# The last gate of a decoder layer: three of its four 256-column blocks by seven products instead of eight

## The chip, the cores and the metric

The kernel runs on one core of a Trainium2 chip. The metric is the device time of one execution in microseconds. The engines are named as the profile names them: PE multiplies matrices, PEld loads its weights, DVE, ACT and POOL (VectorE, ScalarE, GpSimd) work on elements, SP issues the transfers (DMA).

## The reference

One decoder layer on 1024 tokens with model width 1024: a half feed-forward, two gated attention branches, a second half feed-forward, and at the end the gated per-layer input embedding. Only the end is changed:

```python
x = x + 0.5 * swiglu(rms_norm(x, ffn2_norm[i]), ffn2_w_gate[i], ffn2_w_up[i], ffn2_w_down[i])
x = x + jax.nn.sigmoid(rms_norm(x, ple_norm[i]) @ w_ple_gate[i]) * (p[i] @ w_ple_proj[i])
```

All data are float32. `p @ w_ple_proj` is computed early in the kernel and kept in memory as `p_proj`.

## The kernel before

**Precision.** Every float32 operand is split into a high part, which ACT writes by a cast, and a low part, which DVE writes by a subtraction (`split`, L112 and L113, short: hi and lo). A product is three passes of matmuls: hi by hi, lo by hi, hi by lo. One matmul takes 128 rows of the inner dimension, a weight tile of 128 columns and a moving tile of 512 tokens. Activations lie transposed: features on the partitions, tokens in two halves of 512.

**Seven products.** The feed-forward stages already multiply by Strassen's scheme in Winograd's form. A 1024 x 256 block of weights is cut into 2 x 2 pieces, the activations into 2 x 2 (two halves of the inner dimension, two halves of the tokens), and seven products of 12 matmuls replace eight. `product(n, m)` is product m (1 to 7) of block n; I write (n, m) for it. The sums of weight pieces (L462 to L467) are made on POOL or DVE, the sums of activation pieces (`combo_t`, `combo_u`, `combo_d`) on DVE, and their splits (`combo_l`, `combo_s`, `combo_e`) on ACT and DVE. `prep(n, m)` splits the weight operand of a product four products ahead of its use. The results run together in PSUM banks "b" (products 1, 6, 7, 4), "a" (2) and "d" (5, 3), and `evict` copies and adds them.

**Entry of such a stage.** Block 0 is multiplied by eight plain products (`plain`, L449), since the sums of activations aren't there yet; meanwhile the norm of the second half of the tokens is finished and the combinations are made. Then come (1,1), (1,2), (2,1), (2,2) in `products`, and from (1,5) on the list `seqn`. The second feed-forward enters behind the output projection of attention (`second_entry`), whose last chunk of down products has 12 matmuls per tile, as the last chunk of the second feed-forward has.

**The last gate before.** It is plain: 16 units `ple_steps(u)`, each 128 columns by 512 tokens, 24 matmuls at L1591. A unit ends with a sigmoid on ACT (L1594), a multiplication by `p_proj` (L1595) and an addition of the residual X (L1596) on DVE, and a store of 256 KB. Units 0 to 3 use the first half of the tokens, while the norm of the second half is finished beside them. The low parts of the gate's weights are made on POOL (`wlow`, L146). The residual X stays in its two buffers X until the end. The last unit is done in two halves of 256 tokens.

**Order.** From the feed-forward on, the order on each engine is that of the code (`tc.manual_schedule`), each engine works its list in order, and a wait holds up all that stands behind it on that engine. All transfers are issued by SP in one list. Buffers come from pools with a fixed number of slots (GF, RN and PT 3, H 4, KL, KH, Q, Y and X 2), and a new tile waits for a slot's last user.

Of the kernel before, what the change touches and what calls it, by code (L numbers as in the profile page):

```python
# [38 lines left out]
def tile_hybrid_decoder_layer(  # L39
# [360 lines left out]
    def ffn(N, wg, wu, wd, next_gain, resid, hid, tags, entry, tail):  # L400

        wsrc = [kp(w[0]) for w in (wg, wu)]
        wdown = wd[0].rearrange("(j k p) n -> k p j n", k=2, p=P)
        LA = 4
        nm_ = 2 * NF  # L410
# [58 lines left out]
        def prep(n, m):  # L469
            if m == (6 if n == 3 else 1) and n > 2:  # L470
                sums(n, nc.vector if n == 3 else nc.gpsimd)
                if n == 3:
                    last_sum(n)
# [5 lines left out]
            if m == 2 and n > 3:  # L479
# [27 lines left out]

        def evict(n, m, ps):
            up, j = n % 2, n // 2
            if m == 1:  # L510
                E[n] = [slot(t, [P, 2, 512]) for t in (("GF", "RN"), ("Y", "Y"))[up]]
            e1, e2 = E[n]
            if m == 1:
                nc.scalar.copy(e1[:, 0, :], ps[:])
            elif m == 6:
                nc.scalar.copy(e1[:, 1, :], ps[:])
            elif m == 7:
                nc.scalar.copy(e2[:, 1, :], ps[:])
                nc.vector.tensor_add(e2[:, 1, :], e2[:, 1, :], bank_of[n, "d"][:])
            elif m == 2:  # L520
                nc.vector.tensor_add(e1[:, 0, :], e1[:, 0, :], ps[:])
            elif m == 3:
                nc.vector.tensor_add(e1[:, 1, :], e1[:, 1, :], ps[:])
            if not up:
                if m == 7:
                    nc.scalar.activation(e2[:, 1, :], e2[:, 1, :], AF.Silu)
                elif m == 4:
                    nc.scalar.activation(e2[:, 0, :], ps[:], AF.Silu)
                elif m == 3:
                    nc.scalar.activation(e1[:], e1[:], AF.Silu)  # L530
                return
            g1, g2 = E[n - 1]
            if m == 7:
                nc.vector.tensor_mul(g2[:, 1, :], g2[:, 1, :], e2[:, 1, :])
            elif m == 4:
                nc.vector.tensor_mul(g2[:, 0, :], g2[:, 0, :], ps[:])
                nc.sync.dma_start(hid[j, :, 1:3, :], g2[:])
            elif m == 3:
                nc.vector.tensor_mul(g1[:], g1[:], e1[:])
# [1115 lines left out]
```

## Time and profile before

| | us |
|---|---|
| median of 3 runs | 2234.41 (2233.1 to 2235.34) |
| the profiled execution | 2233.62, its span 2231.9 |
| PE / DVE / ACT / POOL busy | 2222.2 / 1489.1 / 970.8 / 811.8 |
| first matmul of the last gate | 2138.14 |
| start of its last two matmuls | 2227.48 |
| first matmul of the second feed-forward (L449) | 1503.00 |

The profile is one execution. Its page gives busy times, the chain of work that ended last, and groups of instructions; the timeline gives instructions in order of time, merged where the same ones follow each other: start, length, engine, line, operation, output and inputs by tile names, count, and in brackets the idle time before and what ended it. ps are PSUM banks, names ending in _dram and p_proj, x_mix, hidden lie in memory. A row of several merged instructions runs from the first one's start to the last one's end; instructions of one engine overlap a little, so the distance from start to start says more than the length.

### The profile page before, as it was taken

What the parts mean: (1) busy time and instruction counts of PE and PEld (TensorE: products, weight loads), DVE (VectorE), ACT (ScalarE), POOL (GpSimd) and SP (SyncE); (2) the same over time, 40 slices, a digit from 0 to 9 for tenths busy, and PEclk for the clock granted to TensorE, in tenths of its full rate; (3) what the DMA queues carried; (4) which work ended last, traced back from release to release, by engine and by line L of the source; (5) the groups of instructions that cost most, each with busy time, mean ns of one, the idle gap of its engine ahead of it and who ended that gap; (6) DMA issues with size and microseconds to landing.
All of it is one profiled execution on the core that took longest, in us unless ns stands there. A gap on an engine that the chain in (4) does not pass through costs nothing.

```text
span 2231.9 us, 29977 instructions
## 1 busy us (share of the span) xinstructions
PE 2222.2 (100%) x11241; PEld 1886.6 (85%) x11241; DVE 1489.1 (67%) x2188; ACT 970.8 (43%) x1694; POOL 811.8 (36%) x709
## 2 busy tenths in 40 slices
PE   9999999999999999999999999999999999999999
PEld 7888888888889999898988888887888888888887
DVE  7955545497894565656666676899654555778873
ACT  6433333343444555545456564255333333434441
POOL 0254444310014656645455654400644443200111
PEclk9999999999999999999999999999999999999999
DMA  8232332474433222222124236741423232655132
GB/s 321 90 123 90 105 108 95 156 286 148 151 129 90 58 86 67 77 62 77 39 71 119 62 124 215 260 143 56 142 94 119 85 128 80 252 201 203 66 118 90
DMA packets 187521, 278.08 MB, mean 125 GB/s; under 512 B 27752, under 2 KB 109928, under 8 KB 187376
## 3 DMA queue, kind: packets, MB, share of 16 engines
q1 hardware_dynamic: 187376, 276.17, 36.8%
q8 instruction: 88, 1.44, 0.3%
q14 instruction: 57, 0.47, 0.1%
HBM read 192.47 MB, written 75.27 MB: 120 GB/s over the span
## 4 chain that ended last, share of the span: by engine, by line
PE 90%; DVE 4%; ACT 2%; issue 2%; DMA 1%; POOL 0%; SPq 0%; DVEq 0%; ACTq 0%; POOLq 0%
PE ps L496 36%; PE ps L388 18%; PE ps L762 11%; PE ps L754 7%; PE ps L1236 4%; PE ps L1591 4%; PE ps L1026 3%; PE ps L1004 2%; PE ps L449 2%; PE ps L953 1%; PE ps L952 1%; ACT H L112 0%; DMA PT<-in_x_tokens_dram 0%; DVE H L113 0%; DVE H L273 0%
## 5 line engine op out<-in xcount | busy, mean ns | idle before, releaser
L388 PE MATMUL ps<-H,H 128*128 128x512 f32 x2184 | 497.3, 389 | 0.0
L388 PEld LDWEIGHTS ps<-H,H 128*128 128x128 f32 x2184 | 409.5, 188 | 84.8
L496 PE MATMUL ps<-H,WL 128*128 128x512 f32 x1008 | 238.9, 389 | 0.0
L496 PEld LDWEIGHTS ps<-H,WL 128*128 128x128 f32 x1008 | 189.2, 188 | 39.3
L762 PE MATMUL ps<-H,WH 128*128 128x512 f32 x768 | 209.5, 401 | 0.0
L762 PEld LDWEIGHTS ps<-H,WH 128*128 128x128 f32 x768 | 136.4, 188 | 22.4
L1007 DVE TENSOR_TENSOR PT<-ps,PT 128x512 fp32r<-128x512 f32 (+1 forms) x160 | 100.4, 633 | 73.7 <-ACT PT L1006 72.8
L146 POOL TENSOR_TENSOR WL<-RAW,WH 128x512 fp32r<-128x512 f32 (+1 forms) x104 | 123.8, 1211 | 63.4 <-ACT WH L136 46.5
L496 PE MATMUL ps<-H,Q 128*128 128x512 f32 x576 | 137.4, 389 | 0.0
L396 DVE SCALAR_TENSOR_TENSOR X<-ps,X 128x512 f32<-128x512 f32 x168 | 108.5, 682 | 41.9 <-PE ps L388 41.8
L754 PE MATMUL ps<-WH,H 128*128 128x256 f32 (+1 forms) x896 | 131.7, 286 | 0.2 <-DVE log_f L793 0.2
L496 PEld LDWEIGHTS ps<-H,Q 128*128 128x128 f32 x576 | 108.1, 188 | 22.4
L1006 ACT CAST PT<-ps 128x512 fp32r<-128x512 f32 (+1 forms) x160 | 86.8, 549 | 85.0 <-PE ps L1004 83.4
L754 PEld LDWEIGHTS ps<-WH,H 128*128 128x128 f32 x896 | 117.2, 190 | 1.1 <-PE ps L754 0.3
L496 PE MATMUL ps<-X,WL 128*128 128x512 f32 x480 | 115.6, 390 | 0.0
L209 POOL TENSOR_TENSOR PT<-PT,RN 128x1024 f32<-128x1024 f32 x2 | 4.8, 2402 | 295.1 <-ACT RN L203 295.1
L762 PE MATMUL ps<-H,WL 128*128 128x512 f32 x384 | 108.7, 399 | 0.0
L1026 PE MATMUL ps<-PT,X 128*128 128x256 f32 (+1 forms) x640 | 106.0, 283 | 1.6 <-DVE PT L1007 1.0
L1026 PEld LDWEIGHTS ps<-PT,X 128*128 128x128 f32 x640 | 95.1, 189 | 14.6 <-DVE PT L1007 4.0
L496 PEld LDWEIGHTS ps<-X,WL 128*128 128x128 f32 x480 | 90.0, 188 | 19.1 <-DVE WL L113 0.5
L965 POOL TENSOR_TENSOR T<-T,l 128x128 f32<-128x128 f32 (+3 forms) x64 | 73.2, 1147 | 85.1 <-DVE l L964 85.1
L496 PE MATMUL ps<-H,PT 128*128 128x512 f32 x432 | 103.2, 390 | 0.2 <-DVE PT L113 0.2
(405 smaller groups left out, 4638.1 us busy)
## 6 DMA issues: line engine op xcount, KB each, us to landing
hidden<-PT SPq DMA_DIRECT2D x40, 512.0 KB, 3.1
WH<-in_ffn_w_gate_dram SPq DMA_DIRECT2D x38, 512.0 KB, 5.4
Q<-hidden SPq DMA_DIRECT2D x24, 512.0 KB, 6.5
hidden<-RN SPq DMA_DIRECT2D x22, 512.0 KB, 2.6
RAW<-in_w_in_dram SPq DMA_DIRECT2D x22, 512.0 KB, 3.9
KH<-in_ffn_w_up_dram SPq DMA_DIRECT2D x20, 512.0 KB, 6.1
KL<-in_ffn_w_up_dram SPq DMA_DIRECT2D x20, 512.0 KB, 6.9
T<-in_ffn_w_down_dram SPq DMA_DIRECT2D x20, 512.0 KB, 4.4
```

Of the source, the lines that this page charges most:

```text
L146: ins = eng_lo.tensor_sub(lo[part], raw[part], f(hi[part]))
L388: pe(nc.tensor.matmul(groups[g][t][:], wt[:, b, k, t * P:(t + 1) * P], act[:, a, k, :], start=(fresh and n == 0), stop=(i in (6, 1, 4) and ...
L396: nc.vector.scalar_tensor_tensor(xs, groups[g][t][:], scale, xs, ALU.mult, ALU.add)
L496: pe(nc.tensor.matmul(ps[:], hl[:, a, k, :], rhs(m, b, k), start=(first and i == 0), stop=(final and i == 11), skip_group_check=True))
L754: pe(nc.tensor.matmul(ps[:, :n], hT[t // 4][a][:, k, (t % 4) * P:(t % 4 + 1) * P], w[k // 4][b][:, k % 4, :n], start=(i == 0), stop=(i == ...
L762: pe(nc.tensor.matmul(ps[:], w[a][:, k, :], hT[half][b][:, k, :], start=(i == 0), stop=(i == 23)))
L965: nc.gpsimd.tensor_mul(T[:, :n], T[:, :n], l[:].broadcast_to([P, n]))
L1006: high = nc.scalar.copy(pt[:, 0, :width], ps[:, :width])
L1007: low = nc.vector.tensor_sub(pt[:, 1, :width], ps[:, :width], f(pt[:, 0, :width]))
L1026: pe(nc.tensor.matmul(o, lh, r, start=(kpair == c and i == 0), stop=(kpair == 0 and i == 3)))
L1236: pe(nc.tensor.matmul(ps[:], w[a][:, k, :], yT[g][b][:, k, half * 512:half * 512 + 512], start=(i == 0), stop=(i == 11)))
L1591: pe(nc.tensor.matmul(ps, pl["w"][d, k // 2][b][:, k % 2, m * P:(m + 1) * P], hT[half][a][:, k, cs], start=(i == 0), stop=(i == 23)))
```

## The change

The code that was inside `ffn` moves into `machine` and `run_products`, with the same order for the feed-forwards. The last gate becomes such a stage with four blocks of 256 columns: block 0 plain, blocks 1 to 3 by seven products, 348 matmuls where there were 384 (the last 24 of them cut in two halves of 256 tokens). It enters with `entry_tail`, the second half of `second_entry`.

The X buffers are needed for the combinations, so the residual is written to memory (`x_last`, eight transfers of 512 KB from `finished`, during the last down products) and read back one 128-column row at a time (`fetch_px`), together with the matching row of `p_proj`. A column d of the result is finished by `finish(i)`, with d = ORDER[i]: a product with `p_proj` and a sum with x, over all 1024 tokens at once; for i = 0 to 3 (columns 0, 1, 2, 4) both are on POOL, for the others on DVE (of column 5 one half on POOL). The weight sums of block 3 move from DVE to POOL. `norm_tags` gives the last down products of the second feed-forward the buffers that the output projection uses.

```diff
+    def machine(N, source, nm_, tags, act):
...
         def prep(n, m):
-            if m == (6 if n == 3 else 1) and n > 2:
-                sums(n, nc.vector if n == 3 else nc.gpsimd)
-                if n == 3:
+            if m == (6 if n == 3 and nm_ > 4 else 1) and n > 2:
+                sums(n, nc.vector if n == 3 and nm_ > 4 else nc.gpsimd)
+                if n == 3 and nm_ > 4:
                     last_sum(n)
...
-            if m == 2 and n > 3:
+            if m == 2 and n > 3 - (nm_ == 4):
                 last_sum(n)
...
+    def sequence(nm_):
+        seqn = [(1, 5), (2, 5), (1, 6), (2, 6), (1, 7), (2, 7), (1, 3), (2, 3), (3, 1), (3, 2), (1, 4), (2, 4), (3, 6), (3, 5), (3, 7)]
+        for n in range(4, nm_ - 1):
+            seqn += [(n, 1), (n - 1, 4), (n, 2), (n - 1, 3), (n, 6), (n, 5), (n, 7)]
+        n = nm_ - 1
+        if n > 3:
+            seqn += [(n, 1), (n - 1, 4), (n, 2), (n, 6), (n, 5), (n, 7), (n - 1, 3)]
+        else:
+            seqn.remove((2, 4))
+            seqn.append((2, 4))
+        seqn += [(n, 3), (n, 4)]
+        return seqn, seqn[:7] + [(1, 4), (2, 3), (3, 1), (3, 2)] + seqn[11:]
...
+    def run_products(M, nm_, evict, each):
+        seqn, seqp = sequence(nm_)
+        for s, (n, m) in enumerate(seqn):
+            evict(n, m, M.product(n, m))
+            if s == 0:
+                for q in range(2):
+                    M.s(q, 7)
+            elif s in (1, 5):
+                M.d(s // 5)
+                M.e(0) if nm_ == 4 and s == 5 else None
+            elif s in (6, 7):
+                M.e(s - 6) if s == 7 or nm_ > 4 else None
+            nxt_ = seqp[s + LA] if s + LA < len(seqn) else None
+            if nxt_:
+                M.prep(*nxt_)
+            each(n, m, nxt_)
...
@@ -713,14 +730,14 @@
                     continue
                 if final:
                     if i == 1:
-                        nxt.extend(norm_begin(X[h], next_gain) for h in range(2))
+                        nxt.extend(tail["begin"](X) if "begin" in tail else [norm_begin(X[h], next_gain) for h in range(2)])
...
+    def entry_tail(F, N):
...
-    def ple_steps(u):
...
+    xf = dp.tile([KD, P, S], F32, name="x_last")
+    def last_gate():
+        G = {"E": {}, "px": {}}
+        tags = {"raw": {0: ("RAW", "RAW"), 1: ("WH", "WH"), 2: ("RAW", "RAW"), 3: ("WH", "WH")}, "sum": {1: "WH", 2: "KL", 3: "WH"}, "w": ("Q", "Q", "KH", "KH"), "hl": ("WL", "WL", "WL", "KL") + ("PT",) * 6 + ("WL", "WL", "PT", "WL", "WL", "PT", "WL", "WL", "WL", "PT", "WL", "WL", "PT", "WL", "WL")}
+        wg = kp(w_ple_gate[0])
+        ORDER = (0, 1, 2, 4, 3, 6, 7, 5)
+        def begin(X):
+            G["x"] = X
+            G["n"] = [combo_begin(X[0], 3, True), combo_begin(X[1], 3, False)]
+            G["m"] = machine(G["n"], lambda n, kh: wg[:, 4 * kh:4 * kh + 4, n * 256:n * 256 + 256], 4, tags, AF.Sigmoid)
+            return G["n"]
+        def finished(half, j):
+            nc.sync.dma_start(xf[2 * j:2 * j + 2, :, half * 512:half * 512 + 512].rearrange("k p n -> p k n"), G["x"][half][:, 2 * j:2 * j + 2, :])
+        def fetch_px(tiles, *order):
+            for i, pair in zip(order, tiles):
+                G["px"][i] = pair
+                for a, src in zip(pair, (pd, xf)):
+                    nc.sync.dma_start(a, src[ORDER[i]].rearrange("p (h n) -> p h n", h=2))
+        def couple(i):
+            return [slot(t, [P, 2, 512])[:] for t in (("GF", "RN"), ("KL", "KL"), ("GF", "RN"), ("KL", "KL"))[i]]
+        def room():
+            t = slot("H", [P, 4, 2, 512])
+            return [(t[:, 2 * j], t[:, 2 * j + 1]) for j in range(2)]
+        def store(d):
+            nc.sync.dma_start(out[:, :, d, :].rearrange("h p n -> p h n"), G["m"].E[d // 2][d % 2][:])
+        def finish(i, parts=((slice(0, 2), slice(0, 512)),)):
+            d = ORDER[i]
+            e = G["m"].E[d // 2][d % 2]
+            a, r = G["px"][i]
+            for h, cs in parts:
+                eng = nc.gpsimd if i in (0, 1, 2, 3) or (i == 7 and h == 1) else nc.vector
+                eng.tensor_mul(e[:, h, cs], e[:, h, cs], a[:, h, cs])
+                eng.tensor_add(e[:, h, cs], e[:, h, cs], r[:, h, cs])
+                if isinstance(h, int):
+                    nc.sync.dma_start(out[h][:, d, cs], e[:, h, cs])
+                elif i not in (2, 3):
+                    store(d)
+            if i < 2:
+                fetch_px([couple(i + 2)], i + 2)
+        def evict(n, m, ps):
+            E, bank_of = G["m"].E, G["m"].bank_of
+            if m == 1:
+                E[n] = [slot(t, [P, 2, 512]) for t in (("GF", "RN"), ("Y", "Y"), ("GF", "RN"), ("KH", "Q"))[n]]
+            e1, e2 = E[n]
+            sig = lambda o, i_: nc.scalar.activation(o, i_, AF.Sigmoid)
+            if m == 1:
+                nc.scalar.copy(e1[:, 0, :], ps[:])
+            elif m == 6:
+                nc.scalar.copy(e1[:, 1, :], ps[:])
+            elif m == 7:
+                nc.scalar.copy(e2[:, 1, :], ps[:])
+                nc.vector.tensor_add(e2[:, 1, :], e2[:, 1, :], bank_of[n, "d"][:])
+                sig(e2[:, 1, :], e2[:, 1, :])
+                if n == 3:
+                    finish(ORDER.index(7), ((1, slice(0, 512)),))
+            elif m == 2:
+                nc.vector.tensor_add(e1[:, 0, :], e1[:, 0, :], ps[:])
+            elif m == 5:
+                if n == 3:
+                    sig(e1[:, 0, :], e1[:, 0, :])
+                    finish(ORDER.index(6), ((0, slice(0, 512)),))
+            elif m == 3:
+                nc.vector.tensor_add(e1[:, 1, :], e1[:, 1, :], bank_of[n, "d"][:])
+                if n == 3:
+                    sig(e1[:, 1, :], e1[:, 1, :])
+                    finish(ORDER.index(6), ((1, slice(0, 512)),))
+                else:
+                    sig(e1[:], e1[:])
+                    finish(ORDER.index(2 * n))
+            elif m == 4 and n < 3:
+                sig(e2[:, 0, :], ps[:])
+                if n == 2:
+                    finish(ORDER.index(5), ((1, slice(0, 512)), (0, slice(0, 512))))
+                else:
+                    finish(ORDER.index(2 * n + 1))
+            elif m == 4:
+                parts = [(0, slice(j * 256, j * 256 + 256)) for j in range(2)]
+                for _, cs in parts:
+                    sig(e2[:, 0, cs], ps[:, cs])
+                finish(ORDER.index(7), parts)
+        def each(n, m, ahead):
+            if (n, m) == (1, 5):
+                finish(0)
+            elif (n, m) == (1, 6):
+                finish(1)
+            elif n == 3 and m < 3:
+                fetch_px(room(), 2 * m + 2, 2 * m + 3)
+                store(ORDER[m + 1])
+        def end(X, N):
+            M = G["m"]
+            entry_tail(dict(vars(M), evict=evict), N)
+            for i in range(2):
+                fetch_px([couple(i)], i)
+            run_products(M, 4, evict, each)
+        hooks = {"begin": begin, "late": True, "end": end}
+        def hook(i, t, call):
+            hooks.setdefault((i, t), []).append(call)
+        for i in (1, 4, 5, 6):
+        return hooks
...
     tags = {"raw": {0: ("RAW", "RAW"), 1: ("WH", "WH"), 2: ("RAW", "RAW"), 3: ("WH", "WH"), 4: ("KH", "KL")}, "sum": {1: "WH", 2: "KL", 3: "KL"}, "w": ("Q", "Q", "KH", "KH"), "hl": ("WL", "WL", "WL", "KL") + ("PT",) * 6 + ("WL", "WL", "PT", "WL", "WL", "PT", "WL", "WL", "WL", "PT", "WL", "Q", "Q")}
-    ffn(N, ffn2_w_gate, ffn2_w_up, ffn2_w_down, 3, xm, ad[1], tags, second_entry, tail)
-    for u in range(8, 16):
-        run(ple_steps(u))
+    ffn(N, ffn2_w_gate, ffn2_w_up, ffn2_w_down, 3, xm, ad[1], tags, second_entry, last_gate())
```

On POOL, this is what stood in the last gate before, from the first low parts of the gate's weights on: only subtractions at L146, two halves to a row, and the two powers of the norms.

```order
L146 TENSOR_TENSOR WL_2676_18242<-Y_2669_18170,WH_2675_18240 128x512 x2
L146 TENSOR_TENSOR WL_2678_18247<-Y_2670_18172,WH_2677_18245 128x512 x2
L248 TENSOR_TENSOR rs_2687_18350<-ss_2686_18345,mhalf_84 128x4
L146 TENSOR_TENSOR GF_2696_18417<-RAW_2683_18317,T_2692_18392 128x512 x2
L146 TENSOR_TENSOR RN_2697_18420<-RAW_2684_18319,T_2693_18394 128x512 x2
L248 TENSOR_TENSOR rs_2709_18542<-ss_2708_18537,mhalf_84 128x4
L146 TENSOR_TENSOR WL_2733_18737<-Y_2723_18665,WH_2732_18735 128x512 x2
L146 TENSOR_TENSOR GF_2735_18753<-Y_2724_18667,T_2734_18751 128x512 x2
L146 TENSOR_TENSOR RN_2739_18775<-RAW_2727_18699,T_2738_18773 128x512 x2
L146 TENSOR_TENSOR PT_2741_18791<-RAW_2728_18701,PT_2740_18789 128x512 x2
```

Now, from the power of the second norm to the end of column 4's sum: L1614 and L1615 are the products and sums of columns 0, 1, 2 and 4, with GF, RN and KL as fetched operands; L445 to L450 are the weight sums of block 3.

```order
L248 TENSOR_TENSOR rs_2699_18523<-ss_2698_18521,mhalf_84 128x4
L1614 TENSOR_TENSOR GF_2695_18513<-GF_2695_18513,GF_2736_18752 128x1024
L1615 TENSOR_TENSOR GF_2695_18513<-GF_2695_18513,RN_2737_18753 128x1024
L1614 TENSOR_TENSOR RN_2696_18514<-RN_2696_18514,KL_2738_18756 128x1024
L1615 TENSOR_TENSOR RN_2696_18514<-RN_2696_18514,KL_2739_18757 128x1024
L445 TENSOR_TENSOR WH_2755_18887<-WH_2751_18845 128x512
L446 TENSOR_TENSOR WH_2751_18845<-WH_2751_18845,WH_2752_18846 128x4x128
L447 TENSOR_TENSOR WH_2755_18887<-WH_2751_18845 128x512
L1614 TENSOR_TENSOR Y_2718_18612<-Y_2718_18612,GF_2743_18784 128x1024
L1615 TENSOR_TENSOR Y_2718_18612<-Y_2718_18612,RN_2744_18785 128x1024
L450 TENSOR_TENSOR WH_2752_18846<-WH_2752_18846,WH_2755_18887 128x4x128
L1614 TENSOR_TENSOR GF_2724_18650<-GF_2724_18650,KL_2748_18825 128x1024
```

The four subtractions per half of the weights are gone, and eight operations on 128 x 1024 elements stand there, the first four ahead of the weight sums of block 3.

On SP before, in the middle of the gate: rows of `p_proj`, the weights of the second 512 columns, and stores.

```order
L1576 DMA KL_2712_18578<-p_proj_88 128x2x512
L1597 DMA out_0_dram<-Q_2713_18580 128x512
L1597 DMA out_0_dram<-KH_2718_18624 128x512
L1576 DMA KL_2720_18657<-p_proj_88 128x2x512
L126 DMA Y_2723_18665<-in_w_ple_gate_dram 128x2x512
L126 DMA Y_2724_18667<-in_w_ple_gate_dram 128x2x512
L1597 DMA out_0_dram<-Q_2721_18659 128x512
L126 DMA RAW_2727_18699<-in_w_ple_gate_dram 128x2x512
```

Now, from the first fetched row to the weights of block 3 (WH): each row of `p_proj` with its row of `x_last`, and the stores of columns 0 and 1.

```order
L1596 DMA GF_2736_18752<-p_proj_88 128x1024
L1596 DMA RN_2737_18753<-x_last_13398 128x1024
L1596 DMA KL_2738_18756<-p_proj_88 128x1024
L1596 DMA KL_2739_18757<-x_last_13398 128x1024
L1606 DMA out_0_dram<-GF_2695_18513 128x2x512
L1596 DMA GF_2743_18784<-p_proj_88 128x1024
L1596 DMA RN_2744_18785<-x_last_13398 128x1024
L1606 DMA out_0_dram<-RN_2696_18514 128x2x512
L1596 DMA KL_2748_18825<-p_proj_88 128x1024
L1596 DMA KL_2749_18826<-x_last_13398 128x1024
L413 DMA WH_2751_18845<-in_w_ple_gate_dram 128x4x256
L413 DMA WH_2752_18846<-in_w_ple_gate_dram 128x4x256
```

The weights of block 3 stand behind four fetched pairs and two stores. In the list of waits KL_2739 takes the slot of KL_2738 and waits for the product of column 1 on POOL, the store of RN_2696 waits for column 1's sum on POOL, and KL_2749 waits for the low part WL_2746 on DVE.

On DVE before, the gate had a product and a sum per unit:

```order
L1595 TENSOR_TENSOR Q_2713_18580<-Q_2713_18580,KL_2702_18494 128x512
L1596 TENSOR_TENSOR Q_2713_18580<-Q_2713_18580,X_2525_16991 128x512
L273 TENSOR_TENSOR H_2654_18024<-PT_2716_18602,H_2653_18023 128x1024
L273 TENSOR_TENSOR H_2654_18024<-Q_2717_18614,H_2653_18023 128x1024
L1595 TENSOR_TENSOR KH_2718_18624<-KH_2718_18624,KL_2702_18494 128x512
L1596 TENSOR_TENSOR KH_2718_18624<-KH_2718_18624,X_2525_16991 128x512
```

Now, in the stretch of (1,5) to (2,7), from the last sum of activations of `combo_u(1)` on: L113 are low parts (WL_2734 of (1,6), H_2731 of the activations of m = 6, WL_2735 of (2,6), X_2741 of m = 7, PT_2742 of (1,7), WL_2746 of (2,7)), L450 weight sums, L537 and L538 `combo_d(0)`.

```order
L528 TENSOR_TENSOR KH_2715_18576<-KH_2715_18576,RN_2683_18378 128x1024
L113 TENSOR_TENSOR WL_2734_18742<-WH_2726_18653,WL_2734_18742 128x512
L113 TENSOR_TENSOR H_2731_18708<-KH_2715_18576,H_2731_18708 128x1024
L113 TENSOR_TENSOR WL_2735_18747<-KL_2729_18678,WL_2735_18747 128x512
L450 TENSOR_TENSOR WH_2692_18465<-WH_2692_18465,WH_2726_18653 128x4x128
L450 TENSOR_TENSOR RAW_2702_18530<-RAW_2702_18530,KL_2729_18678 128x4x128
L113 TENSOR_TENSOR X_2741_18773<-Q_2705_18552,X_2741_18773 128x1024
L113 TENSOR_TENSOR X_2741_18773<-Q_2714_18573,X_2741_18773 128x1024
L113 TENSOR_TENSOR PT_2742_18778<-WH_2726_18653,PT_2742_18778 128x512
L537 TENSOR_TENSOR Q_2705_18552<-H_2652_18023,KH_2707_18558 128x1024
L538 TENSOR_TENSOR Q_2705_18552<-Q_2705_18552,H_2652_18023 128x1024
L113 TENSOR_TENSOR WL_2746_18803<-KL_2729_18678,WL_2746_18803 128x512
```

All of them stand in one list, and the low parts of (1,7) and (2,7) come behind the combinations for m = 6, 7 and 4.

More of the change, by code (lines that the diff above doesn't have):

```diff
@@ L506, in right @@
             return t[:, b, k, :]
[L508 to L539, printed above, removed]
-                nc.sync.dma_start(hid[j, :, 0, :], g1[:, 0, :])
-        def hidden_sums(n, tags):
-            j = n // 2
-            block_sums(hid[j], *E[n - 1], tags)
-            del E[n], E[n - 1]
         C = {}
```

145 lines of the change are left out of this document (62 added, 83 removed).

## Prediction

> **What bounds it now.** The page first: PE is busy over the whole span.
>
> ```profile
> PE 2222.2 (100%) x11241; PEld 1886.6 (85%) x11241; DVE 1489.1 (67%) x2188; ACT 970.8 (43%) x1694; POOL 811.8 (36%) x709
> ```
>
> So what counts is how many matmuls the gate has and whether PE waits. The windows compare the gate (second row) with the entry of the second feed-forward (first row), which the changed gate copies. In the gate DVE is busy 40.7 of 89.9 us; in the entry 58.31 of 62.00, and POOL does nothing there (1.01).
>
> ```profile
> 1503.00:1565.00 62.00, 61.41 (x269) 48.92 (x268) 58.31 (x74) 31.33 (x47) 1.01 (x1) 1.00 0.25 79
> 2138.10:2228.00 89.90, 89.04 (x417) 73.91 (x416) 40.70 (x53) 23.72 (x40) 12.64 (x9) 1.00 0.35 116
> ```
>
> Then PE's timeline in the gate, from its first matmul to its last two.
>
> ```profile
> 2138.14 1.07 PE L1591 MATMUL ps<-H,WH 128*128 128x512 f32 x4
> ...
> 2140.40 0.74 PE L1591 MATMUL ps<-H,T 128*128 128x512 f32 x2 [0.74 <-ACT H L270]
> ...
> 2156.69 1.07 PE L1591 MATMUL ps<-H,WH 128*128 128x512 f32 x4
> ...
> 2162.13 1.07 PE L1591 MATMUL ps<-H,WH 128*128 128x512 f32 x4
> ...
> 2227.48 0.40 PE L1591 MATMUL ps<-H,PT 128*128 128x256 f32 x2
> ```
>
> A unit of 24 matmuls takes 2162.13 - 2156.69 = 5.44 us, one matmul 0.227. The gate lasts from 2138.14 to 2227.88, 89.7 us, with one wait of 0.74.
>
> **Matmuls.** The changed gate is the entry of the second feed-forward, row for row, as far as (1,5), and then 17 products of 12 matmuls. PE's timeline there:
>
> ```profile
> 1503.00 2.88 PE L449 MATMUL ps<-H,WL 128*128 128x512 f32 x12
> 1506.27 3.22 PE L449 MATMUL ps<-H,WL 128*128 128x512 f32 x12 [0.39 <-ACT WL L112]
> ...
> 1522.89 4.98 PE L496 MATMUL ps<-H,PT 128*128 128x512 f32 x20 [0.20 <-DVE PT L113]
> ...
> 1538.60 5.60 PE L496 MATMUL ps<-H,PT 128*128 128x512 f32 x24
> 1544.04 5.60 PE L496 MATMUL ps<-H,WL 128*128 128x512 f32 x24
> 1549.47 2.88 PE L496 MATMUL ps<-X,PT 128*128 128x512 f32 x12
> 1552.19 3.02 PE L496 MATMUL ps<-X,WL 128*128 128x512 f32 x12
> 1555.05 5.63 PE L496 MATMUL ps<-T,WL 128*128 128x512 f32 x24
> ```
>
> I count t from the gate's first matmul, which answers to 1503.00. (1,5) starts at t = 35.6, its waits of 0.39 and 0.20 included; 17 products of 2.72 (1552.19 - 1549.47) are 46.2; with 0.2 for the last one's end the gate lasts 82.0. That is **7.7 us less** than 89.7; the old wait of 0.74 and the copied ones of 0.59 are in the two lengths, and so are the norm's transposes, as many in each. The eight stores to x_last cost nothing: the stores to x_mix stand at the same places in front of 1503.00, and PE waits there no longer than shown; without that cover the first loads of weights, which stand behind them in SP's list, would be late. The fetched rows of x add 4 MB to the gate's transfers, beside 116 GB/s in the window above, and their room is DMA share 0.35 of 1; what they cost is the wait for each, below.
>
> **GpSimd and VectorE.** The term that decides. Rows of POOL and DVE where both work:
>
> ```profile
> 2084.88 2.40 POOL L209 TENSOR_TENSOR PT<-PT,RN 128x1024 f32<-128x1024 f32 x1 [147.54 <-ACT RN L203]
> ```
>
> ```profile
> 2085.78 3.73 DVE L113 TENSOR_TENSOR H<-Y,H 128x1024 fp32r<-128x1024 f32 x2 [2.12 <-ACT H L112]
> 2089.44 2.35 DVE L113 TENSOR_TENSOR H<-Q,H 128x1024 fp32r<-128x1024 f32 x2
> ```
>
> ```profile
> 1573.51 0.68 DVE L536 TENSOR_TENSOR RN<-RN,ps 128x512 f32<-128x512 f32 x1
> ...
> 1576.91 1.78 DVE L113 TENSOR_TENSOR WL<-WH,WL 128x512 fp32r<-128x512 f32 x1
> 1578.61 1.77 DVE L113 TENSOR_TENSOR WL<-KL,WL 128x512 fp32r<-128x512 f32 x1
> ```
>
> ```profile
> 1576.39 1.75 POOL L286 TENSOR_TENSOR PT<-RN,PT 128x512 f32<-128x512 f32 x1
> 1578.10 1.73 POOL L462 TENSOR_TENSOR RAW<-KH 128x512 f32<-128x512 f32 x1
> ```
>
> Two DVE operations take 2.35 alone and 3.73 when they start beside POOL's sum of 128 x 1024: 1.38 more, about what was left of that sum (2087.28 - 2085.78 = 1.50). Against POOL's operations of 512 they go by turns, one DVE operation of 0.6 and one POOL operation of 1.1 to a period of 1.7. The operation that reads a PSUM bank takes 0.68 all the same. I read: with both operands in SBUF, DVE stands still while POOL works, less 0.1; by turns. A POOL operation on 1024 elements costs a loaded DVE **2.28 us**. [...]
>
> A POOL product of 128 x 1024 is not in the trace. Its length: below, the 1.29 of a sum of 512 alone; above, 4.5, two operations of 2.27 beside DVE; I take the 2.40 of L209, the same shape and kinds of operands. Its price to DVE: below nothing, where DVE is idle anyway; above 2.40.
>
> ```profile
> L284 POOL TENSOR_TENSOR PT<-PT,GF x20: 1289/1292/1632, 97.8 to 1899.1; 128x512 f32<-128x512 f32 x20
> ```
>
> ```profile
> L286 POOL TENSOR_TENSOR KL<-RN,KH 128x512 f32<-128x512 f32 x2 | 4.5, 2270 | 0.0
> ```
>
> Now where they fall. DVE's timeline in the copied entry:
>
> ```profile
> 1535.43 1.23 DVE L584 TENSOR_TENSOR KH<-KH,GF 128x1024 f32<-128x1024 f32 x1
> ...
> 1544.14 1.23 DVE L113 TENSOR_TENSOR H<-KH,H 128x1024 fp32r<-128x1024 f32 x1 [0.52 <-ACT H L112]
> ...
> 1549.36 0.68 DVE L113 TENSOR_TENSOR PT<-WH,PT 128x512 fp32r<-128x512 f32 x1
> ...
> 1552.35 0.68 DVE L113 TENSOR_TENSOR WL<-KL,WL 128x512 fp32r<-128x512 f32 x1
> ```
>
> Column 0's row of p_proj is fetched once L584 has freed a GF slot (1536.66, t = 33.7). A fetch is 512 KB:
>
> ```profile
> KL<-p_proj SPq DMA_DIRECT2D x8, 512.0 KB, 4.3
> X<-x_mix SPq DMA_DIRECT2D x8, 512.0 KB, 10.9
> ```
>
> ```profile
> Y<-in_w_ple_gate_dram SPq DMA_DIRECT2D x2, 512.0 KB, 6.2
> ```
>
> I take p_proj's 4.3 (10.9 is for four at once), so POOL's first product starts near t = 38. By turns with DVE, product 0, sum 0 and product 1 end near t = 47.4; only then is column 1's x fetched, into the slot of its p row; sum 1 runs at about 52 to 55. All four stand in front of the low parts of (1,7) and (2,7) on DVE. These are written at 1550.04 and 1553.03, and PE wants them after four matmuls of their products, at 1549.47 + 0.91 = 1550.38 and 1553.10: a slack of 0.3 and 0.1. Four times 2.28 is 9.1; DVE's idle 0.5 and the slack take off 0.7. **PE comes 8.4 us late** to (1,3), t = 60.5 for 52.05.
>
> **Block 3.** Its weights wait in SP's list for sum 1 (t = 55), and behind that for the low part of (2,7) (58.5): issue at 59, landing between 63.3 (4.3) and 65.2 (6.2). PE wants the low part of (3,1) at 66.8. In front of it DVE has, from 61.6, a low part (0.6), a sum from PSUM (0.65), the two of combo_d (2.4), a split of m = 4 (1.15) and its own 0.6, 5.4 together, so 67.0, and one to three of POOL's weight sums come between, 1.1 each (67.8 to 70.4): a wait of 1.0 to 3.6; I take 2.3, since either landing has its row.
>
> ```profile
> 1563.99 1.06 ACT L530 ACTIVATE GF<-GF 128x1024 f32<-128x1024 f32 x1 [4.57 <-DVE GF L523]
> ```
>
> Behind it the three lists hang on each other; I count from L, the end of (3,1)'s low part, so that (3,1) ends at L + 1.8. DVE then adds (1,3)'s PSUM (0.7), ACT makes its sigmoid (1.06) and after it (3,2)'s high part (0.6): L + 2.3, PE waits 0.5. That sigmoid has released POOL's product of column 2, at L + 1.8, so (3,2)'s low part is done at L + 4.7 where PE wants it at 3.2: 1.4. DVE's sum for (2,3), its sigmoid and the last high parts of m = 4 (1.05) follow in one chain: 0.5. POOL's product of column 4 starts behind the last low part of m = 4 and blocks (3,6)'s: 1.5. Its sum blocks (3,5)'s: 0.2. Column 3's two DVE operations stand ahead of (2,4)'s low part: 0.4. With the 2.3, **6.8 us** (5.5 to 8.1).
>
> **Tail.** Before, the last 256 columns pass once through ACT and twice through DVE.
>
> ```profile
> 2227.92 0.38 ACT L1594 ACTIVATE KH<-ps 128x256 f32<-128x256 f32 x1 [2.49 <-PE ps L1591]
> ```
>
> ```profile
> 2228.33 0.43 DVE L1595 TENSOR_TENSOR KH<-KH,KL 128x256 f32<-128x256 f32 x1 [1.99 <-ACT KH L1594]
> 2228.79 0.43 DVE L1596 TENSOR_TENSOR KH<-KH,X 128x256 f32<-128x256 f32 x1
> ```
>
> Now PE's last product ends both halves at once, and the second half waits for the first one's two DVE operations: **0.9 more**. The store behind it is the same.
>
> **Sum.** -7.7 + 8.4 + 6.8 + 0.9 = +8.4 us on the profiled execution's 2233.62, so 2242.0. The median of the runs is 0.8 higher; on it, 2242.8.
>
> **Rivals.** (a) POOL catches DVE only in the full stretch: behind (1,3) DVE has fewer operations than the copied entry (its two products of gate and up are gone), and PE waits no more. For it speaks that DVE was busy only 40.7 of 89.9 us in the old gate, against it that the three lists release each other there. -7.7 + 8.4 + 0.9 = +1.6: 2236.0.
>
> (b) The other side, faster: the lock costs little, because DVE's operations slip between POOL's. The place is the stretch from t = 38 to 55, the price the 2.28 per operation. For it: some DVE operations beside POOL are shorter than 1.7 in that timeline. What decides: the stalls must stay under 7.7 - 0.9 = 6.8 us to gain anything, under 0.9 us per POOL operation when all eight count as they do here. With none, only the weights of block 3 are late: column 1's sum is done at 51.4, the weights land near 57.2, and (3,1) waits 0.3. -7.7 + 0.9 + 0.3 = -6.5: 2227.9.
>
> (c) The fetch of column 1's x takes 10.9 instead of 4.3: sum 1, the store and the weights of block 3 slip by up to 6.6, of which 3 to 4 reach PE beyond the forecast: 2246.5.
>
> **Chances.** Forecast 0.58, (a) 0.20, (b) 0.17, (c) 0.05. About 0.2%, 4.5 us, is what a measurement of this kernel can tell from no change. Slower: forecast and (c), 0.63; same: (a), 0.20; faster: (b), 0.17. The forecast by itself spans 2239 to 2246 (its bounds of 5.5 and 8.1, and 2 us for the 8.4, where the first fetch may take from 4.3 to 6.2). The range leaves out (b) and the upper part of (c): 2230 to 2247.
>
> **What would show it.** Right: POOL's L1614 and L1615 of 1024 elements at 2.4 to 3.5 us; DVE's L113, L527 and L528 between t = 38 and 55 at 1.8 to 3.5; PE waiting for DVE's L113 at (1,6), (1,7), (3,1), (3,2) and (3,6), 8 us before (1,3) and some 7 behind. Wrong: (1,3) at t = 52 to 54, or DVE's operations there at 0.68 and 1.22. If PE waits for ACT at (3,1) with the weights of block 3 as releaser, it is SP's list, not the lock. If the gate's matmuls alone don't come to 79 us, the first term is wrong.

## The result, and the profile after

The changed kernel takes 2245.97 us (2245.05 to 2247.86) where the kernel before takes 2234.24 beside it: ratio 1.0054, 95% interval 1.0041 to 1.0067, so 11.7 us slower. The forecast was 2242.8. The profiled execution took 2246.67, its span 2245.0.

The page's first part:

```profile
PE 2221.5 (99%) x11181; PEld 1880.2 (84%) x11181; DVE 1540.3 (69%) x2231; ACT 986.7 (44%) x1716; POOL 820.6 (37%) x707
```

PE has 60 matmuls fewer (36, and the old gate's last 24 were cut in two), yet is busy only 0.7 us less in a span that is 13.1 longer. The windows of the gate, as before: length, then busy time of PE, PEld, DVE, ACT, POOL, and behind them PE's granted clock, DMA share and GB/s. Rows: up to (1,5); (1,5) to (2,7); from (1,3) on.

```profile
2138.60:2174.20 35.60, 35.04 (x154) 27.27 (x153) 33.74 (x46) 17.72 (x25) 1.01 (x1) 1.00 0.29 96
2174.20:2198.60 24.40, 18.73 (x73) 14.07 (x72) 24.07 (x19) 9.04 (x15) 11.87 (x4) 0.93 0.54 193
2198.60:2240.00 41.40, 35.10 (x133) 26.40 (x132) 33.79 (x29) 15.01 (x24) 21.80 (x10) 0.92 0.54 197
```

The first row is the copied entry, 35.6 us as forecast. In the second, six products that need 16.3 take 24.4, DVE is busy for 24.07 of it and POOL for 11.87. In the third, eleven that need 30.1 take 41.4, and in both the granted clock is below 1 (0.93 and 0.92). PE's timeline there:

```profile
2179.63 0.61 PE L479 MATMUL ps<-H,WL 128*128 128x512 f32 x2
2183.98 0.73 PE L479 MATMUL ps<-H,WL 128*128 128x512 f32 x2 [3.73 <-ACT H L112]
2185.68 6.15 PE L479 MATMUL ps<-H,WL 128*128 128x512 f32 x20 [0.97 <-DVE WL L113]
2191.67 1.07 PE L479 MATMUL ps<-X,PT 128*128 128x512 f32 x4
2193.71 2.11 PE L479 MATMUL ps<-X,PT 128*128 128x512 f32 x8 [0.97 <-DVE PT L113]
...
2198.66 5.64 PE L479 MATMUL ps<-T,WL 128*128 128x512 f32 x24
2204.14 1.07 PE L479 MATMUL ps<-H,WL 128*128 128x512 f32 x4
2208.27 6.80 PE L479 MATMUL ps<-H,WL 128*128 128x512 f32 x20 [3.06 <-DVE WL L113]
2214.91 3.37 PE L479 MATMUL ps<-X,PT 128*128 128x512 f32 x12
2218.12 1.09 PE L479 MATMUL ps<-H,PT 128*128 128x512 f32 x4
2220.36 2.11 PE L479 MATMUL ps<-H,PT 128*128 128x512 f32 x8 [1.14 <-DVE PT L113]
...
2232.67 4.60 PE L479 MATMUL ps<-T,WL 128*128 128x512 f32 x12 [1.97 <-DVE Q L1635]
2237.11 2.89 PE L479 MATMUL ps<-X,WL 128*128 128x512 f32 x12
```

The waits stand at (1,6), (1,7), (3,1) and (3,6), as forecast; the (3,2) of the forecast shows as slow clock instead, and there is one more wait, at (3,3), 2232.67. The longest, 3.73 at (1,6), ends with a cast on ACT, which had itself stood 6.87 waiting for DVE's L528. (1,3) starts 60.04 us after the gate's first matmul at 2138.62; 60.5 was forecast. There is also something that the forecast doesn't have: 20 matmuls need 4.53 and 12 need 2.72, but the 20 at 2185.68 take 5.99 to the next row, the 20 at 2208.27 take 6.64, and the 12 of (3,3) take 4.44.

DVE and POOL at the start of it:

```profile
2176.14 3.41 DVE L527 TENSOR_TENSOR Q<-KH,Q 128x1024 f32<-128x1024 f32 x1
2179.59 3.26 DVE L528 TENSOR_TENSOR KH<-KH,RN 128x1024 f32<-128x1024 f32 x1
2182.78 2.85 DVE L113 TENSOR_TENSOR WL<-WH,WL 128x512 fp32r<-128x512 f32 x1
...
2188.49 4.56 DVE L113 TENSOR_TENSOR X<-Q,X 128x1024 fp32r<-128x1024 f32 x2
```

```profile
2175.90 2.58 POOL L1614 TENSOR_TENSOR GF<-GF,GF 128x1024 f32<-128x1024 f32 x1 [28.29 <-DMA GF<-p_proj]
2178.55 3.21 POOL L1615 TENSOR_TENSOR GF<-GF,RN 128x1024 f32<-128x1024 f32 x1
2181.73 3.35 POOL L1614 TENSOR_TENSOR RN<-RN,KL 128x1024 f32<-128x1024 f32 x1
2189.20 2.77 POOL L1615 TENSOR_TENSOR RN<-RN,KL 128x1024 f32<-128x1024 f32 x1 [4.12 <-DMA KL<-x_last]
2201.61 1.64 POOL L445 TENSOR_TENSOR WH<-WH 128x512 f32<-128x512 f32 x1 [9.64 <-DMA WH<-in_w_ple_gate_dram]
```

DVE's four instructions beside POOL's four are longer by 2.19, 2.04, 2.17 and 2.21 than alone (1.22, 1.22, 0.68, 2.35). The first three end 1.07, 1.09 and 0.55 behind the end of the POOL instruction beside them, which is nearly their own length: DVE gets hardly anything done until POOL's instruction ends, and then runs at its own pace.

The account from profiled execution to profiled execution: the gate needs 82.0 without losses, 7.7 less than before; it loses 8.15 before (1,3), 11.25 behind it, and ends 101.4 after its start; the end behind PE is 5.0 instead of 4.0; and all that stands ahead of the gate took 0.5 longer in this execution (in the runs below the gate starts between 2137.2 and 2138.9). -7.7 + 8.15 + 11.25 + 1.0 + 0.5 = 13.2, for 13.05 measured. The medians are 11.7 apart.

### The profile page after: what moved, and what is told of

Read it like the earlier page. It is cut to its first block, busy times and chain, and to the rows that moved or that the text cites. A ratio compares the mean times of both kernels' runs of the same rounds, so it can differ in the third digit from the quotient of the medians.

```text
span 2245.0 us, 29947 instructions
## 1 busy us (share of the span) xinstructions
PE 2221.5 (99%) x11181; PEld 1880.2 (84%) x11181; DVE 1540.3 (69%) x2231; ACT 986.7 (44%) x1716; POOL 820.6 (37%) x707
## 4 chain that ended last, share of the span: by engine, by line
PE 90%; DVE 5%; issue 2%; ACT 2%; DMA 1%; SPq 0%; DVEq 0%; ACTq 0%
PE ps L479 36%; PE ps L388 20%; PE ps L779 11%; PE ps L771 7%; PE ps L1253 4%; PE ps L1043 3%; PE ps L1021 2%; PE ps L432 2%; PE ps L970 1%; PE ps L969 1%; PE ps L1303 1%; DVE X L113 1%; DVE WL L113 1%; ACT T L980 0%; DVE T L974 0%
## 5 line engine op out<-in xcount | busy, mean ns | idle before, releaser
L479 PE MATMUL ps<-H,WL 128*128 128x512 f32 x1068 | 257.1, 393 | 7.8 <-DVE WL L113 4.0
L479 PEld LDWEIGHTS ps<-H,WL 128*128 128x128 f32 x1068 | 202.2, 190 | 51.9 <-DVE WL L113 5.6
L146 POOL TENSOR_TENSOR WL<-RAW,WH 128x512 fp32r<-128x512 f32 (+1 forms) x104 | 123.9, 1213 | 63.4 <-ACT WH L136 46.6
L479 PE MATMUL ps<-H,PT 128*128 128x512 f32 x516 | 123.8, 391 | 1.6 <-DVE PT L113 1.6
L479 PE MATMUL ps<-X,WL 128*128 128x512 f32 x516 | 124.5, 390 | 0.0
L479 PEld LDWEIGHTS ps<-H,PT 128*128 128x128 f32 x516 | 96.3, 188 | 24.0 <-DVE PT L113 4.2
L479 PEld LDWEIGHTS ps<-X,WL 128*128 128x128 f32 x516 | 96.6, 188 | 20.9 <-DVE WL L113 0.9
L779 PE MATMUL ps<-H,WL 128*128 128x512 f32 x384 | 108.8, 399 | 0.0
```

The lines of the kernel that those rows point to most:

```text
L146: ins = eng_lo.tensor_sub(lo[part], raw[part], f(hi[part]))
L479: pe(nc.tensor.matmul(ps[:], hl[:, a, k, :], rhs(m, b, k), start=(first and i == 0), stop=(final and i == 11), skip_group_check=True))
L779: pe(nc.tensor.matmul(ps[:], w[a][:, k, :], hT[half][b][:, k, :], start=(i == 0), stop=(i == 23)))
```

## Experiments

The theory: DVE stands still while POOL reads SBUF, and PE waits for DVE. Rival Q: DVE's list is too long by itself. Rival S: the weights of block 3 come late by SP's list. Rival D: the slow clock of PE is a loss of its own. All in one table: t(1,3) and t(3,4) are starts, counted from the gate's first matmul in the profiled execution; without any loss they would be 51.9 and 79.1. Each has the kernel before from the same chip beside it.

| run | t(1,3) | t(3,4) | median us | before |
|---|---|---|---|---|
| the change | 60.04 | 98.49 | 2245.97 | 2234.24 |
| e1_no_finish | 52.01 | 82.21 | 2231.36 | 2233.48 |
| e2_no_finish_24 | 60.02 | 90.21 | 2239.61 | 2233.48 |
| e3_finish_dve | 58.47 | 91.62 | 2239.20 | 2233.48 |
| e4_weights_early | 60.03 | 94.94 | 2242.42 | 2233.28 |
| e5_spare_matmuls | 60.04 | 97.33 | 2244.68 | 2233.48 |
| e7_pool_memset | 52.00 | 84.21 | 2232.07 | 2233.28 |
| e8_pool_copy | 54.66 | 86.98 | 2233.73 | 2233.28 |
| v1_dve_late | 52.06 | 83.86 | 2237.58 | 2233.28 |
| v2_dve_filled | 52.00 | 86.89 | 2237.68 | 2234.17 |
| v3_fetch_first | 52.05 | 82.58 | 2231.97 | 2233.34 |

**Without POOL's products and sums.**

```diff
+                if i > 3:
                     eng.tensor_mul(e[:, h, cs], e[:, h, cs], a[:, h, cs])
                     eng.tensor_add(e[:, h, cs], e[:, h, cs], r[:, h, cs])
```

> Left out: the products with p_proj and the sums with the residual of columns 0, 1, 2 and 4 (the eight POOL operations of 128x1024); their fetches and stores stay. Theory (VectorE stands still while GpSimd works on SBUF operands): the stretch (1,5) to (2,7) loses nothing, so (1,3) starts 52 to 52.5 us after the gate's first matmul instead of 60.0; the weight sums of block 3 and the half of column 5 stay on POOL, so 0.5 to 2.5 us of waits stay behind (1,3), too short for the clock to dip; 2228 (2226.5 to 2231). Rival Q (VectorE's list is too long by itself, whatever POOL does): the list is the same, 2245. Rival S (the weights of block 3 come late by SP's list): only the wait at (3,1) goes, (1,3) stays at 60, 2240.

(1,3) starts at 52.01, with DVE's list the same: rival Q is out, and all 8.15 of the first stretch is POOL's four operations. Behind it one wait is left, at (3,1):

```profile
2195.41 1.07 PE L479 MATMUL ps<-H,WL 128*128 128x512 f32 x4
2198.56 5.25 PE L479 MATMUL ps<-H,WL 128*128 128x512 f32 x20 [2.08 <-DVE WL L113]
```

It is what POOL's weight sums cost (DVE's 1.22 and 0.68 beside them take 2.31 and 1.74, 2.15 more together). The time came 3.4 above the forecast's middle and just out of its range; the profiled execution, at 2229.67, was the shortest of ten.

**Without those of columns 2 and 4 alone**: the same edit with `if i not in (2, 3):`.

> Left out: products and sums of columns 2 and 4 alone (four POOL operations). Theory: (1,3) still at 60.0 and the wait at (3,1) of 3.2 with the slow clock behind it as in the changed kernel, since both lie ahead of column 2's product; the losses at (3,2), (1,4), (3,6) and (3,3), together about 6, go for the most part: 2240 (2238.5 to 2242.5). Rival Q: no change, 2246. If (1,3) moves too, the theory's places are wrong.

The time and (1,3), at 60.02, are as expected, and the losses at (3,6) and (3,3) are gone, those at (3,2) and (1,4) but for 0.5 and 0.2. The wait at (3,1) is not: it is 2.1 instead of 3.2, with no slow clock behind it.

**The same operations on DVE.**

```diff
-                eng = nc.gpsimd if i in (0, 1, 2, 3) or (i == 7 and h == 1) else nc.vector
+                eng = nc.gpsimd if i == 7 and h == 1 else nc.vector
...
```

> The same eight operations on VectorE instead of GpSimd (column 1's sum one product later, since it waits for its fetch). Theory: each costs VectorE its own 1.2 us instead of the 2.3 and more for which it stands still, so the first stretch loses about 4 instead of 8 ((1,3) at 56), the second about 5 to 7 instead of 11: 2239 (2235 to 2242). Rival Q: VectorE's list becomes 9.8 us longer, 2252 to 2256.

The time is the forecast's. With the eight operations DVE's list is longer, and the kernel is still 6.8 us faster than with the shorter list beside POOL. t(1,3) was off, 58.5 for 56: DVE waits 1.83 for column 1's x, and the sum that frees the bank for (1,3) stands behind that.

**Spare matmuls in PE's waits** (bank "av", free in the gate).

```diff
+                    at, count = {(1, 6): (2, 14), (3, 1): (4, 12), (3, 3): (0, 8)}.get((n, m), (0, 0)) if nm_ == 4 else (0, 0)
+                    if i == at and count:
+                        spare = bank("av")
+                        for _ in range(count):
+                            pe(nc.tensor.matmul(spare[:], hl[:, 0, 0, :], rhs(m, 0, 0), start=True, stop=True, skip_group_check=True))
```

> The changed kernel with 34 spare matmuls into an unused PSUM bank, 14 ahead of the third matmul of (1,6), 12 ahead of the fifth of (3,1), 8 ahead of (3,3), each no longer than the wait that stood there (3.7, 3.2 and 2.1 us). Theory D (the granted clock falls to 0.5 for some 3.4 us after PE stood still for 2 us or more): the three dips go, 1.5 + 1.8 + 1.7 = 5 us less, 2241 (2240 to 2243). Rival (the clock falls for another reason, or the matmuls are simply more work): 2246 or more.

The windows of the change, one us each, at the three places (the number behind POOL's is the granted clock), and then the same places with spare matmuls:

```profile
2187.00:2188.00 1.00, 1.00 (x4) 0.71 (x4) 1.00 (x3) 0.39 (x1) 0.00 (x0) 0.50 0.79 217
2210.00:2211.00 1.00, 1.00 (x4) 0.79 (x3) 0.55 (x1) 0.41 (x1) 1.00 (x1) 0.50 0.00 0
2234.00:2235.00 1.00, 1.00 (x4) 0.81 (x3) 0.97 (x3) 0.00 (x0) 0.00 (x0) 0.50 0.00 0
```

```profile
2184.00:2188.00 4.00, 3.24 (x14) 2.72 (x15) 4.00 (x6) 3.56 (x6) 0.15 (x1) 1.00 0.64 202
2207.00:2211.00 4.00, 3.30 (x12) 2.10 (x12) 2.37 (x3) 1.57 (x2) 1.91 (x1) 1.00 0.10 25
2232.00:2236.00 4.00, 4.00 (x20) 3.30 (x19) 3.36 (x5) 0.83 (x3) 0.00 (x0) 1.00 0.36 134
```

All three stretches at half clock are gone, so PE's standing still makes them. But 5 us did not come of it: the last product starts 1.2 earlier in the gate (97.33 for 98.49), and the 1.3 between the medians are within the noise. (1,3) starts at 60.04 as before: where the slow clock at (1,6) is gone, PE waits 2.28 at (1,7) for DVE's low part instead of 0.97. In front of DVE's list a slow PE costs nothing here. Only behind the last low part, at (3,3), does it count; there the eight spare matmuls end 0.7 after DVE's sum (2232.30 and 2231.62), so that 1.7 of slow clock gives back only 1.2.

**Weights of block 3 earlier.**

```diff
-            if m == (4 if 0 < n < 3 else 3) and n + 2 < nm_:
+            if m == (4 if 0 < n < 3 and (n, nm_) != (1, 4) else 3) and n + 2 < nm_:
```

> The weights of block 3 are issued ahead of column 1's store and column 4's fetches, so they land some 3 us earlier in SP's list. Theory (VectorE held by GpSimd): at (3,1) VectorE comes late because two of block 3's weight sums on POOL stand between, wherever they run; within 1.5 us of the changed kernel, 2246 (2244.5 to 2247). Rival S (SP's list makes the weights late): the wait of 3.2 at (3,1) shrinks by 3, 2242 to 2243.

My theory was wrong here and rival S right: 3.5 us less (as much in the gate, 94.94 for 98.49), and the wait at (3,1) falls from 3.1 to 0.70.

```profile
2203.89 1.07 PE L479 MATMUL ps<-H,WL 128*128 128x512 f32 x4
2205.65 3.39 PE L479 MATMUL ps<-H,WL 128*128 128x512 f32 x12 [0.70 <-DVE WL L113]
```

```profile
2197.16 1.29 POOL L445 TENSOR_TENSOR WH<-WH 128x512 f32<-128x512 f32 x1 [5.97 <-DVE PT L113]
2198.53 1.29 POOL L446 TENSOR_TENSOR WH<-WH,WH 128x512 f32<-128x512 f32 x1
2199.91 1.61 POOL L447 TENSOR_TENSOR WH<-WH 128x512 f32<-128x512 f32 x1
```

The sums now run from 2197.2 to 2201.5, where DVE waits 1.21 for ACT and reads PSUM, instead of beside three instructions in line that end with (3,1)'s low part. (1,4) starts 1.9 earlier; the rest is (3,3), where PE waits 1.0 and the clock stays whole. So it is both: DVE is held by POOL, and SP's list settles which of its instructions are.

**What of POOL's work holds DVE: fills and copies** in the place of each product and sum.

```diff
+                    eng.memset(e[:, h, cs], 0.5)
+                    eng.memset(e[:, h, cs], 0.25)
```

```diff
+                    eng.tensor_copy(e[:, h, cs], a[:, h, cs])
+                    eng.tensor_copy(e[:, h, cs], r[:, h, cs])
```

> Left out: the products and sums of columns 0, 1, 2 and 4; in the place of each stands a POOL fill of 128x1024 with a constant, which writes SBUF and reads nothing. Theory L (what stops VectorE is that POOL reads SBUF): VectorE's operations beside the fills keep 0.7 and 1.2, (1,3) at 52 to 53, about as without them, 2231 (2229 to 2233). Rival A (any work of POOL on SBUF stops VectorE): VectorE's operations there last 2 to 3, (1,3) late by about the fills' own time.

> As the run with fills, but a POOL copy of 128x1024 from the fetched row instead, which reads one operand and not two. Theory L: a copy stops VectorE for its own length, as a sum does; (1,3) late by four times the copy's length less about 1. Rival B (two readers share a bandwidth, so one operand less costs half): VectorE's operations beside the copies last at most half as much more as beside the sums.

Fills first: POOL, then DVE at the same time.

```profile
2173.61 0.96 POOL L1618 MEMSET RN<- 128x1024 f32 x1 [3.42 <-ACT RN L440]
2174.63 0.95 POOL L1619 MEMSET RN<- 128x1024 f32 x1
```

```profile
2172.78 1.22 DVE L113 TENSOR_TENSOR H<-KH,H 128x1024 fp32r<-128x1024 f32 x1
2174.09 0.69 DVE L113 TENSOR_TENSOR PT<-RAW,PT 128x512 fp32r<-128x512 f32 x1
2174.70 1.22 DVE L527 TENSOR_TENSOR Q<-KH,Q 128x1024 f32<-128x1024 f32 x1
```

Nothing is longer beside a fill, and (1,3) starts at 52.00. (They run earlier than the products, since they wait for no fetch, but DVE is working without a gap there too.) Copies, POOL and DVE:

```profile
2176.42 1.92 POOL L1619 COPY GF<-RN 128x1024 f32<-128x1024 f32 x1
2203.91 1.04 POOL L1618 COPY Y<-GF 128x1024 f32<-128x1024 f32 x1 [2.30 <-ACT Y L1632]
```

```profile
2175.38 2.06 DVE L527 TENSOR_TENSOR Q<-KH,Q 128x1024 f32<-128x1024 f32 x1
2177.47 1.94 DVE L528 TENSOR_TENSOR KH<-KH,RN 128x1024 f32<-128x1024 f32 x1
```

A copy takes 1.04 undisturbed and holds DVE for 0.84 and 0.72; a product takes 2.4 and holds it for 2.0 to 2.2. (1,3) is late by 2.7, within the 3.1 that theory L gives. The price was POOL's own time, less 0.2 to 0.3, for one operand as for two, and nothing beside fills of 0.96, which only write. Rival B's bound (at most half as much) would be 1.1, so 0.84 alone can't rule it out. The ends speak against it: DVE's second instruction, 1.22 long by itself, ends 1.07 behind the end of the second copy, as its instructions do behind the products, so hardly any of it was done while the copy ran; by rival B more would have been. With fills and with copies the wait at (3,1) stays at 3.1 and 3.2: there POOL's weight sums, which are left as they are, meet the same three instructions as in the change.

**Can the order be mended?** All on DVE, the products of the first columns behind the low parts of block 3, weights and rows fetched earlier.

```diff
-                eng = nc.gpsimd if i in (0, 1, 2, 3) or (i == 7 and h == 1) else nc.vector
+                eng = nc.vector
...
+                if (n, m) == (2, 7):
+                    load(3)
...
+            elif (n, m) == (3, 1):
+                fetch_px(room(), 2, 3)
+                finish(0)
+            elif (n, m) == (3, 2):
+                fetch_px(room(), 4, 5)
+                finish(1)
...
```

> Computes all. Every product and sum, and block 3's weight sums, on VectorE; columns 0, 1, 2 and 4 are finished behind the low parts of (3,6) to (2,4) instead of ahead of them, the weights of block 3 are fetched earlier, rows of later columns in H. Theory: without POOL, VectorE has 53 us of work in the gate from (1,5) on, PE 46; the low parts come first, so PE waits less than 2 us, and VectorE is done 3 to 5 us later after PE's end than in the changed kernel: 2231 (2229 to 2234). Rival Q (VectorE's list is too long whatever POOL does): 2250 or more.

Missed by 6.6. PE's one long wait is at (3,6), 1.9 with the slow clock behind it, since block 3's sums came just ahead of it. But DVE stood still 1.2, 1.6 and 2.1 us waiting for ACT's casts with work at hand, and ended 8.7 behind PE (2.1 in the change). The next version puts that work there, `between` being called behind the evictions of (1,7), (1,3) and (2,3):

```diff
+        def between(s):
+            if s == 4:
+                G["m"].sums(3, nc.vector)
+            else:
+                finish(s - 6)
...
```

> Computes all. As v1_dve_late, but the products and sums of columns 0 and 1 and the weight sums of block 3 stand where VectorE was idle in v1_dve_late (1.2, 1.6 and 2.1 us, waiting for ScalarE), so the sums are there before (3,6) wants them. Theory (VectorE's own work sets the end): PE loses about 2 us in all and no dip, VectorE ends some 5 us earlier than in v1_dve_late, 2232.5 (2231 to 2235), no faster than the kernel before by more than 0.1%, since VectorE then works nearly without a gap from (1,5) to its last sum. Rival (what is left in v1_dve_late is PE's waits, not VectorE's work): PE's 4.4 us of loss go and the time falls by 4.4 and no more, 2233.2, with VectorE's end still 8 us behind PE's.

No faster: rival and theory both missed. DVE now waits for fetched rows, which stood in SP's list behind the stores of columns 0 and 1:

```profile
2209.55 1.22 DVE L1621 TENSOR_TENSOR Y<-Y,H 128x1024 f32<-128x1024 f32 x1 [1.92 <-DMA H<-p_proj]
...
2224.48 0.69 DVE L1621 TENSOR_TENSOR Q<-Q,H 128x512 f32<-128x512 f32 x1 [2.81 <-DMA H<-p_proj]
```

The last version issues the fetches first:

```diff
             elif (n, m) == (3, 1):
                 fetch_px(room(), 2, 3)
+                store(0)
...
```

> Computes all. As v2_dve_filled, but each group of fetched rows is issued ahead of the stores of finished columns, on which it waited in SP's list (6.3, and up to 8 us). Theory F (what v2_dve_filled lost behind (1,4) was VectorE waiting for those fetches, 6.8 us in six waits): VectorE waits less than 2 us for transfers, PE's wait of 2.9 at (3,3) and the slow clock behind it go, VectorE ends 4 to 6 us earlier, 2232.5 (2230.5 to 2235), level with the kernel before. Rival G (the transfers themselves, 400 GB/s, are the limit): they end no earlier, 2236 to 2238.

Theory F holds: 2231.97, ratio 0.9995 (0.9986 to 1.0004) to the kernel before, 14 us less than the change and with the same matmuls. Its gate:

```profile
2137.70:2223.20 85.50, 83.43 (x357) 64.81 (x355) 82.03 (x104) 41.60 (x63) 1.01 (x1) 1.00 0.49 176
```

DVE is busy 82.03 of 85.5 us and then another 3.6 to its last sum, with POOL out of the way. That is where this gate ends: the matmuls saved are 7.7 us, of which PE's losses take back 3.5 (82.58 for 79.1) and the longer end behind PE 3.0 (7.0 for 4.0), both behind a DVE that hardly stands still. No version that computes everything beats the kernel before by more than can be told from none.

## Why the prediction was right, point by point

The direction, the place and the price were right; the size, 8.4 us slower forecast and 11.7 measured, came out low by one term, (3,3) below. Rival (c) with 2246.5 lies nearer to the 2245.97 than the forecast's 2242.8, but by chance, since what it rests on did not happen.

- **Matmuls, -7.7: right.** (1,5) starts 35.57 after the first matmul, and a product without a wait takes 2.72 (e1_no_finish has it from (3,6) to the end).
- **The first stretch, +8.4: right**, 8.15, and shown by e1_no_finish to be POOL's. The times of day hold too: first product at 37.3 (38 forecast), column 1's sum from 50.6 to 53.4 (52 to 55). The single price was 2.0 to 2.2 for 2.28. A part of the 8.15, 1.5, shows as slow clock and not as wait; e5_spare_matmuls shows that the sum is DVE's either way.
- **(3,1), +2.3 within 1.0 to 3.6: right within its bounds**, 3.2. (By the terms named there the bounds are 1.3 and 3.5.) "either landing has its row" understated the landing: three of the sums met three instructions in line, and with the weights 3 us earlier most of it was gone.
- **The steps behind, +4.5: right one by one up to (2,4)**, 4.2 in all: 2.1 from (3,1)'s fifth matmul to (1,4) for (3,2) (1.9 forecast), 0.5 at (1,4) (0.5), 1.46 at (3,6) (1.5), 0.1 at (3,5) (0.2), 0 at (2,4) (0.4).
- **The term that was missing: (3,3), 3.85 us.** (3,3) goes on in the bank that DVE's sum for (3,7) reads (L1635), and that sum stands behind two low parts held by POOL's half of column 5, and behind column 6. I followed the low parts and left this bank out: 2.1 are lost ahead of it. The 1.7 of slow clock behind it is the one stretch at half clock that cost time, and the forecast has no clock at all. This one step is most of the difference between +8.4 and +13.05 in the profiled executions. DVE there, beside POOL's product of column 5, which is followed by its sum at 2227.92:

```profile
2226.61 1.78 DVE L113 TENSOR_TENSOR PT<-RAW,PT 128x512 fp32r<-128x512 f32 x1
2228.31 1.77 DVE L113 TENSOR_TENSOR WL<-WH,WL 128x512 fp32r<-128x512 f32 x1
...
2231.93 0.68 DVE L1635 TENSOR_TENSOR Q<-Q,ps 128x512 f32<-128x512 f32 x1
```

```profile
2225.79 2.05 POOL L1614 TENSOR_TENSOR RN<-RN,H 128x512 f32<-128x512 f32 x1 [3.24 <-DMA H<-p_proj]
```

e2_no_finish_24 keeps POOL's half of column 5 and loses nothing at (3,3): without the operations of columns 2 and 4 DVE has written these low parts before that half starts.

- **Tail, +0.9: right**, 1.0.
- **Rivals.** (a) and (b) are out: DVE is caught in both stretches, and each POOL product or sum of 128 x 1024 costs it nearly POOL's whole time (2.0 to 2.2 of 2.4). (c) did not happen: column 1's x landed 4.1 after its issue at 2185.11.
- **The cause: right as far as it went.** That DVE, with both operands in SBUF, stands still while POOL works holds in the change. The runs with fills and copies add that it was POOL's reading of SBUF that did it here: 0 for a fill, 0.72 to 0.84 for a copy of 1.04.

## What to carry to other kernels

Before moving elementwise work to GpSimd, ask how busy VectorE is in that stretch: where it was full of work on SBUF operands here, each GpSimd product or sum of 128 x 1024 cost it nearly that operation's own length (2.0 to 2.2 us of 2.4), while the same operation on VectorE took 1.2. Fewer matmuls pay only as far as the engines that prepare them have room: count their work in the shortened stretch first. And a wait of PE is not yet a price: what it costs is read from when the engine behind it would have been done.

## What was not expected of the hardware

PE's granted clock fell to 0.50 when it stood still, in the change for 3.41 us each time (windows of 0.1 us: 2185.10 to 2188.51, 2208.99 to 2212.40, 2232.88 to 2236.29), and for longer in the first slow stretch of e2_no_finish_24, e3_finish_dve and e4_weights_early: at least 5.1, 6.0 and 5.8, estimated from how long the matmuls behind the wait take. It did so with waits of 3.7, 3.1 and 2.0 us in the change and 1.9 in v1_dve_late, and not with 2.1 in e1_no_finish and e2_no_finish_24 or 2.3 in e5_spare_matmuls, so the length alone doesn't settle it, and the expectation of e1_no_finish, that waits up to 2.5 are too short for a dip, holds for that run and not for the change.

The three starts in the change are 23.9 apart, 7 times 3.41, and a fourth one behind PE's end, at 2243.12, is 10.24 after the third, 3 times 3.41: the four starts of this run lie on a grid of 3.41 us. On it the wait of 2.0 at (3,3) (2230.7 to 2232.7) lies whole within one step (2229.5 to 2232.9). In e2_no_finish_24 the first slow stretch ends at about 2189.35 (estimated: the 20 matmuls from 2185.95 on take 1.70 longer than 4.53, so 3.40 at half clock); five steps on is 2206.4, which cuts the wait of 2.1 (2205.4 to 2207.6) in two, and no slow stretch follows. So the place of a wait on the grid may decide; two waits don't show that it does.

A POOL copy of 128x1024, which reads one operand, took 1.04 in e8_pool_copy (at 2203.91). A POOL product of the same size, which reads two, took 2.37 in the change (at 2209.98, begun before the DVE instruction beside it), more than twice as long. Why is not shown.
